# Smaller TensorE parts for two sets of products, and one multiplication on ScalarE instead of GpSimd, in a hybrid RWKV-7 / HGRN2 step

## The chip, the cores and the metric

The kernel runs on one core of one Trainium2 chip. The metric is the time of one execution on the device in microseconds (us). The core has five engines with queues of their own: TensorE (PE, its weight loads are shown apart as PEld), VectorE (DVE), ScalarE (ACT), GpSimd (POOL) and SyncE (SP), which issues the transfers.

## The reference, cut to what matters

One layer serves a prompt of 256 tokens and 8 samples of 8 tokens each, so 320 columns of tokens in all. A combined projection of the normalised input feeds an RWKV-7 branch (16 heads of 64) and an HGRN2 branch (8 heads of 128). The change lies in the two recurrences:

```
# HGRN2, per head: S_t = diag(g_t) S_{t-1} + k_t v_t^T,   o_t = S_t^T q_t
att = einsum('nhtd,nhsd,nhtsd->nhts', qc, kc, decay_ts)       # causal, decayed q.k products
o   = einsum('nhtd,nhde->nhte', qc * exp(b), s) + einsum('nhts,nhse->nhte', att, vc)
s   = exp(b_last)[..., None] * s + einsum('nhsd,nhse->nhde', kc * exp(b_last - b), vc)

# RWKV-7, per head: S_t = S_{t-1} diag(w_t) - (S_{t-1} kk_t)(kk_t * a_t)^T + v_t k_t^T,  y_t = S_t r_t
```

After the layer come a gated merge, an output projection, a residual and a final norm. Both groups' new states are outputs too.

## The kernel before

The channels lie on partitions and the tokens on the free dimension. Large projections are made of float32r products of 128x128 weights with 320 tokens; each weight block (128 columns of 1024 rows) is loaded from memory, cast to its high part on ScalarE (`whi`) and its low part is subtracted on VectorE (`wlo`), and 8 x 3 products use it (`mps`). Weights have three buffers.

From 29 to 718 us of the execution a recorder is at work. `record_all` writes down all operations of 68 projection tiles (3264 `mps` products), of 8 RWKV pairs (`rwkv`, two heads each) and of 8 HGRN heads (`hgrn`). `Recorder.order` then plans the order for each engine from estimated costs, with `mps` products between the small ones, and replays it; in the trace all of it has the line of the replay, L1396, so places are told by their tiles. Small products in PSUM tiles `a` belong to `rwkv`, those in `b` to `hgrn`. They are float32 products, and the trace shows each as two passes, so two rows per product. After 718 us the remaining projections follow, untouched by the change.

Of `rwkv` the change touches the pair products (lines 868 to 878): for each of four 64-token chunks of the prompt, and for the samples, one product of `bk2[:, ci]` (128 channels of two heads by 128 columns) with `arp[:, ci]` (256 columns: for each head a part that is zero in the other head's 64 rows). VectorE multiplies them by a mask into `g2`.

Of `hgrn` it touches the attention scores inside the prompt (lines 1168 to 1267). Blocks of 8 tokens have scores of their own (`k0`, `q0`), and levels of 8, 16, 32 and 64 tokens join neighbouring blocks (`level(sz)` gives one `kq` tile). `products` makes 128x128 products of which only the parts near the diagonal count:

```
for j in range(2):
    tk_ = slice(128 * j, 128 * j + 128)
    T.matmul(ps[:, o_ + 128 * j:o_ + 128 * j + 128], kq[:, tk_], q_[:, tk_], start=True, stop=True)
```

`keep` copies the parts into `att` under a mask (`copy_predicated`). The samples have a product of 64 columns of their own. Their old states `s0` (128x1024 per head) meet the queries in 8 products with 32 columns each (`qz`, lines 1221 to 1224), four of which fill the array side by side. Then line 1245 multiplies `s0` by the decay `dec` on GpSimd in one operation, line 1252 adds the new part, and line 1253 stores it from SP's queue, behind which weight loads wait.

Of the kernel before, what the change touches and what calls it, by code (L numbers as in the profile page):

```python
# [9 lines left out]
F32 = mybir.dt.float32  # L10
F32R = mybir.dt.float32r
U8 = mybir.dt.uint8
# [5 lines left out]
NP_ = 256  # L18
# [30 lines left out]
class Op:  # L49
    __slots__ = ("eng", "fn", "args", "kw", "cost", "lat", "uses", "mode", "passes", "cols", "stream",  # L50
                 "succ", "npred", "ready", "rank", "block", "margin", "wait", "port", "hold", "dma", "n")

# [16 lines left out]
class Recorder:  # L69
# [3 lines left out]
    def __init__(self, engines, is_big):  # L73
        self.real, self.ops, self.spans, self.is_big = engines, [], {}, is_big
        self.block, self.wait = None, 0

# [8 lines left out]
    def add(self, eng, name, fn, args, kw):  # L85
# [18 lines left out]
        o.mode = None  # L104
        o.block = self.block
        o.margin, o.wait = 0, self.wait
# [4 lines left out]
        if eng == "PE":  # L111
# [12 lines left out]
            stream = n / 2.4 + 13 if one and lhs.dtype == F32R else 2 * n / 2.4  # L124
            o.cost = o.passes * max(load, stream / min(2, 128 // o.mode[1]))
            if o.mode == (128, 128) and n > 256:
# [27 lines left out]
    def link(self):  # L154

        writers, readers = {}, {}
        for o in self.ops:
            o.succ, pred = [], {}
            for name, p0, p1, m, wr, psum in o.uses:
# [22 lines left out]
            o.npred = len(pred)  # L182
            for q, data in pred.values():
                q.succ.append((o, data))
        for o in reversed(self.ops):
            o.rank = o.cost + max((q.rank + (o.lat if data else 0) for q, data in o.succ), default=0)

    def order(self):
# [85 lines left out]
def hybrid_step(ctx, tc, x_prompt, x_sample, state_rwkv, state_hgrn, state_shift, norm_g, w_in,  # L274
# [19 lines left out]
    def ctile(shape, name, dt=F32, pool=rconst):  # L294
        return pool.tile(shape, dt, name=name, tag=name)
# [59 lines left out]
    with tc.tile_pool(name="start", bufs=1) as st, \  # L355
# [100 lines left out]

        mf = st.tile([64, 3, 64], F32, name="mf")
        mu8 = ctile([128, 3, 64], "mu8", U8)
        G.memset(mf, 1.0)
        for n, sz in enumerate((8, 8, 16)):  # L460
            if n == 0:
                mfh = mf[:, 0].rearrange("p (b i) -> p b i", i=8)
                keep_ge(mf[:, 0], [[1, 64]], 0, -1)
                keep_ge(mfh, [[-8, 8], [0, 8]], 0, 1)
                keep_ge(mfh, [[8, 8], [0, 8]], 7, -1)
                continue
            lv = mf[:, n].rearrange("p (b two s) -> p b two s", two=2, s=sz)
            nb = 32 // sz
# [3 lines left out]
        for sl in HS:  # L472
            G.tensor_copy(mu8[sl], mf)

# [210 lines left out]
    def ring(pool, tag, shape, bufs, dt, size, clear=False):  # L685
# [12 lines left out]
        if len(shape) == 2:  # L698
# [4 lines left out]
    SIZES = {"uK": 384, "uS": 384, "uE": 384, "uA": 320, "uB": 384, "uQ": 320, "big": 512, "s0t": 512, "v": 384,  # L703
             "w1": 384, "w2": 320, "w3": 320, "ks": 128, "ket": 256}


    CLEAR = {"uB", "uE", "ys", "rhs", "rhs2", "k3", "vm", "w1", "vt"}

# [50 lines left out]
    def rwkv(p, r, k, vp, za):  # L759
# [107 lines left out]
        M = at("M", (128, 3, 2, 64), tag="uE")  # L867
        for g in range(3):
            ps = aps("pg")
            n = 2 if g < 2 else 1  # L870
            for c_ in range(n):
                ci = 2 * g + c_
                T.matmul(ps[:, 256 * c_:256 * c_ + 256], bk2[:, ci].rearrange("p j t -> p (j t)"),
                         arp[:, ci].rearrange("p x h t -> p (x h t)"), start=True, stop=True)
            m = mk[:, 0:2] if g < 2 else mk[:, 2:3]
            V.tensor_mul(g2[:, 2 * g:2 * g + n].rearrange("p c x h t -> p (c x) h t"),
                         ps[:, :256 * n].rearrange("p (a h t) -> p a h t", h=2, t=64),
                         m.rearrange("p c x t -> p (c x) t")[:, :, None].to_broadcast([128, 2 * n, 2, 64]))

# [245 lines left out]
    def hgrn(hd, q, k, v, zb):  # L1125
# [42 lines left out]
        att = bt("att", (128, 2 * 128 + 64))  # L1168
        G.memset(att, 0.0)

        def level(sz, tag):
            half = lambda t_: t_[:, :NP_].rearrange("p (b two s) -> p b two s", two=2, s=sz)
            kq = bt("kq", (128, NP_), tag=tag)
            if sz in (32, 64):

                side = [kq[:, 128 * x:128 * x + 128].rearrange("p (b s) -> p b s", s=sz) for x in range(2)]
            else:
                side = [half(kq)[:, :, x] for x in range(2)]
            for x, e in enumerate((R, F)):
# [9 lines left out]


        def products(ps, o_, kq, q_):
            for j in range(2):
                tk_ = slice(128 * j, 128 * j + 128)
                T.matmul(ps[:, o_ + 128 * j:o_ + 128 * j + 128], kq[:, tk_], q_[:, tk_], start=True, stop=True)

        def keep(ps, o_, n):
            own = lambda t_, c_: t_.rearrange("p (j c t) -> p j c t", c=2, t=64)[:, :, c_]
            for c_ in range(2):
                sl = HS[c_]
                V.copy_predicated(own(att[sl, :NP_], c_), mu8[sl, None, n].to_broadcast([64, 2, 64]),  # L1200
                                  own(ps[sl, o_:o_ + NP_], c_))

        kq8 = level(8, "w2")
        ps = bps("pg")
        products(ps, 0, k0, q0)
        products(ps, 256, kq8, kq8)
        keep(ps, 0, 0)
        keep(ps, 256, 1)

# [10 lines left out]
        ps = bps("pos")  # L1220
        for si in range(NSEQ):
            j = si % 4
            T.matmul(ps[32 * j:32 * j + 32, 128 * (si // 4):128 * (si // 4) + 128], qz[:, si, :], s0[:, si, :],
                     start=True, stop=True)
        sot = bt("sot", (128, 256), tag="ket")
        S.copy(sot, ps[:, :256])
        ps = bps("pke")
        T.matmul(ps[:, 128:192], k0[:, NP_:], q0[:, NP_:], start=True, stop=True)
        T.transpose(ps[0:64, :128], es[:, 1], ident)
        V.copy_predicated(att[0:64, NP_:], mu8[0:64, 0], ps[0:64, 128:192])  # L1230
        k3 = bt("k3", (128, 2, 128), dt=F32R)
# [30 lines left out]
        for j in range(2):  # L1262
            for b in range(2):
                o_ = 64 * j + 32 * b
                V.tensor_copy(att[64 * b:64 * b + 32, 128 * j + 64 * b + 32:128 * j + 64 * b + 64],
                              ps[o_:o_ + 32, 256 + o_:288 + o_])
            V.tensor_copy(att[0:64, 128 * j + 64:128 * j + 128], ps[HS[j], 384 + 64 * j:448 + 64 * j])

# [42 lines left out]
    def shift_state():  # L1311
        for g, (s_, n) in enumerate(((0, 5), (5, 4))):
# [265 lines left out]
```

## Time and profile before

| | us |
|---|---|
| median of 3 runs (1156.60 to 1157.67) | 1157.26 |
| the profiled execution | 1155.96 |
| its span | 1154.3 |
| PE busy | 1135.7 (98%) |
| DVE busy | 775.9 (67%) |
| ACT busy | 669.2 (58%) |
| POOL busy | 208.0 (18%) |

Busy time is an average over the stages, and matmuls overlap in the records, so what a product costs is read from the distance between the starts of the records around it. "Idle before" and the waits tell what an engine waited for. TensorE's granted clock is 1.00 (2.4 GHz) in the whole stretch that the change touches.

### The profile page before, as it was taken

The numbers are of one execution on the slowest core, as the hardware profiler recorded it, in microseconds if no ns is written. First come the engines' busy times: TensorE is split into PE (matmuls) and PEld (weight loads), VectorE is DVE, ScalarE is ACT, GpSimd is POOL, SyncE is SP. The second block draws the span as 40 slices with busy tenths as digits, with TensorE's granted clock in tenths as the row PEclk, the third lists the DMA queues.
The fourth block names the chain that finished last, engine by engine and source line by source line (L and its number), as shares of the span: only waits on it lengthen the run. The fifth ranks groups of instructions, "written<-read, shape, count | busy, mean of one in ns | idle before, by whom it ended". The sixth has DMA issues, their size and how long they took to land.

```text
span 1154.3 us, 20774 instructions
## 1 busy us (share of the span) xinstructions
PE 1135.7 (98%) x7816; PEld 1097.9 (95%) x7816; DVE 775.9 (67%) x1634; ACT 669.2 (58%) x1483; POOL 208.0 (18%) x405
## 2 busy tenths in 40 slices
PE   6999999999999999999999999999999999999997
PEld 6999999999999999999999999999999999998886
DVE  8778878877887888878788686544444444436632
ACT  6766766667666667567667667444444444435322
POOL 9432223222311321421321310000000000000000
PEclk9999999999999999999999999999999999999999
DMA  6745435535445435436435434555555555577512
GB/s 180 199 117 127 129 102 136 142 92 132 129 113 146 117 93 150 131 81 169 120 93 162 115 105 132 148 152 153 152 147 148 151 154 151 146 253 254 182 41 91
DMA packets 283096, 159.69 MB, mean 138 GB/s; under 512 B 22893, under 2 KB 273264, under 8 KB 282356
## 3 DMA queue, kind: packets, MB, share of 16 engines
q1 hardware_dynamic: 282996, 158.37, 48.6%
q8 instruction: 61, 1.00, 0.4%
q14 instruction: 39, 0.32, 0.1%
HBM read 148.53 MB, written 9.81 MB: 137 GB/s over the span
## 4 chain that ended last, share of the span: by engine, by line
PE 96%; POOL 2%; DVE 1%; ACT 1%; issue 0%; DMA 0%; ACTq 0%; POOLq 0%
PE mps L1396 41%; PE a L1396 13%; PE mps L338 6%; PE mps L340 6%; PE mps L339 6%; PE b L1396 4%; PE po L1479 3%; PE po L1481 3%; PE po L1480 3%; PE ppb L338 2%; PE ppa L338 2%; PE ppb L340 2%; PE ppa L340 2%; PE ppa L339 2%; PE ppb L339 2%; PE po L1484 1%
## 5 line engine op out<-in xcount | busy, mean ns | idle before, releaser
L1396 PE MATMUL mps<-hhi,wlo 128*128 128x320 f32 x1088 | 344.9, 317 | 0.0
L1396 PE MATMUL mps<-hlo,whi 128*128 128x320 f32 x1088 | 344.7, 317 | 0.0
L1396 PE MATMUL mps<-hhi,whi 128*128 128x320 f32 x1088 | 344.6, 317 | 0.0
L1396 PEld LDWEIGHTS mps<-hlo,whi 128*128 128x128 f32 x1088 | 204.9, 188 | 3.3 <-issue 3.0
L1396 PEld LDWEIGHTS mps<-hhi,wlo 128*128 128x128 f32 x1088 | 205.0, 188 | 2.7 <-issue 2.4
L1396 PEld LDWEIGHTS mps<-hhi,whi 128*128 128x128 f32 x1088 | 205.0, 188 | 0.8 <-issue 0.4
L329 DVE TENSOR_TENSOR wlo<-raw,whi 128x1024 fp32r<-128x1024 f32 x88 | 107.8, 1225 | 125.0 <-ACT whi L328 124.8
L328 ACT CAST whi<-raw 128x1024 fp32r<-128x1024 f32 x88 | 92.3, 1048 | 163.3 <-PE mps L339 104.8
L1396 ACT CAST whi<-raw 128x1024 fp32r<-128x1024 f32 x134 | 140.6, 1049 | 77.2 <-PE mps L1396 75.8
L1396 DVE TENSOR_TENSOR wlo<-raw,whi 128x1024 fp32r<-128x1024 f32 x134 | 167.5, 1250 | 24.4 <-ACT whi L1396 23.1
L339 PE MATMUL mps<-hlo,whi 128*128 128x320 f32 x448 | 138.5, 309 | 0.0
L338 PE MATMUL mps<-hhi,whi 128*128 128x320 f32 x448 | 138.5, 309 | 0.0
L340 PE MATMUL mps<-hhi,wlo 128*128 128x320 f32 x448 | 138.5, 309 | 0.0
L340 PEld LDWEIGHTS mps<-hhi,wlo 128*128 128x128 f32 x448 | 84.1, 188 | 0.0
L338 PEld LDWEIGHTS mps<-hhi,whi 128*128 128x128 f32 x448 | 84.1, 188 | 0.0
L339 PEld LDWEIGHTS mps<-hlo,whi 128*128 128x128 f32 x448 | 84.1, 188 | 0.0
L1468 DVE TENSOR_TENSOR wlo<-raw,whi 128x1024 fp32r<-128x1024 f32 x32 | 38.5, 1222 | 39.1 <-ACT whi L1467 39.0
L1467 ACT CAST whi<-raw 128x1024 fp32r<-128x1024 f32 x32 | 33.1, 1051 | 48.4 <-DMA raw<-in_w_out_dram 22.4
L1479 PE MATMUL po<-whi,mhi 128*128 128x512 f32 x128 | 50.1, 391 | 0.7 <-DVE gbt L1436 0.7
L1481 PE MATMUL po<-wlo,mhi 128*128 128x512 f32 x128 | 50.0, 391 | 0.0
L1480 PE MATMUL po<-whi,mlo 128*128 128x512 f32 x128 | 50.0, 391 | 0.0
L339 PE MATMUL ppb<-ybl,whi 128*128 128x320 f32 x128 | 39.6, 309 | 0.0
(409 smaller groups left out, 2304.0 us busy)
## 6 DMA issues: line engine op xcount, KB each, us to landing
raw<-in_w_in_dram SPq DMA_DIRECT2D x194, 512.0 KB
raw<-in_w_out_dram SPq DMA_DIRECT2D x32, 512.0 KB
raw<-in_proj_a_dram SPq DMA_DIRECT2D x16, 512.0 KB
raw<-in_proj_b_dram SPq DMA_DIRECT2D x16, 512.0 KB
s<-in_state_hgrn_dram SPq DMA_DIRECT2D x8, 512.0 KB
out_dram<-s SPq DMA_DIRECT2D x8, 512.0 KB
s<-in_state_rwkv_dram SPq DMA_DIRECT2D x8, 256.0 KB
out_dram<-s SPq DMA_DIRECT2D x8, 256.0 KB
```

The lines of the kernel that those rows point to most:

```text
L328: S.copy(hi[:, ks], raw[:, ks])
L329: sub.tensor_sub(lo[:, ks], raw[:, ks], hi[:, ks].bitcast(F32))
L338: T.matmul(dst, hi[:, q, :], xhi[:, k, :], start=(k == 0), stop=False)
L339: T.matmul(dst, hi[:, q, :], xlo[:, k, :], start=False, stop=False)
L340: T.matmul(dst, lo[:, q, :], xhi[:, k, :], start=False, stop=(k == nk - 1))
L1396: o.fn(*o.args, **o.kw)
L1467: S.copy(hi, raw)
L1468: V.tensor_sub(lo, raw, hi.bitcast(F32))
L1479: T.matmul(pt, h, hi, start=first, stop=False)
L1480: T.matmul(pt, l, hi, start=False, stop=False)
L1481: T.matmul(pt, h, lo, start=False, stop=end)
L1484: T.matmul(pt, h, hi, start=first, stop=False)
```

## The change

Three things are done. (1) The scores of all levels are computed in parts of 32 columns (32x32 tiles of scores, 64 wide at the level of 64) right behind the `qz` products, in one group that the planner keeps together (`side_by_side` sets `group`; a member waits for what any member waits for, and all have the highest rank). `products` and `keep` go; the parts of blocks of 8 and levels of 8 and 16 are gathered under masks in a small tile `attc` and copied to `att` by ScalarE. `att` is cleared once for all heads. (2) The pair products of the four chunks are made by head: 64 rows of the array for each head, 128 columns, into one PSUM bank per head, also as a group. (3) `s0` is multiplied by `dec` on ScalarE in 8 operations of 128x128. The planner's cost for a group divides by the tiles that run side by side. The cut diff:

```diff
@@ Recorder.add
+            side = 128 // o.mode[1] * (128 // o.mode[0] if o.group else 1)
+            o.cost = o.passes * max(max(load, stream) / side, 7) if o.group else o.passes * max(load, stream / min(2, side))
@@ Recorder.link
+            for o in members:
+                preds[o.n].update(shared)
...
+            top = max(o.rank for o in members)
@@ rwkv
-        for g in range(3):
-            ps = aps("pg")
-            n = 2 if g < 2 else 1
-            for c_ in range(n):
-                ci = 2 * g + c_
-                T.matmul(ps[:, 256 * c_:256 * c_ + 256], bk2[:, ci].rearrange("p j t -> p (j t)"),
-                         arp[:, ci].rearrange("p x h t -> p (x h t)"), start=True, stop=True)
...
+        banks = [aps("pg") for _ in HS]
+        side_by_side([((banks[h][:, 128 * ci:128 * ci + 128], bk2[HS[h], ci].rearrange("p j t -> p (j t)"),
+                        arp[HS[h], ci, :, h]), dict(start=True, stop=True)) for ci in range(4) for h in range(2)])
...
+        T.matmul(ps[:, :256], bk2[:, 4].rearrange("p j t -> p (j t)"), arp[:, 4].rearrange("p x h t -> p (x h t)"),
+                 start=True, stop=True)
@@ hgrn
-        G.memset(att, 0.0)
-        products(ps, 0, k0, q0)
-        products(ps, 256, kq8, kq8)
-        keep(ps, 0, 0)
-        keep(ps, 256, 1)
+        kq8, kq16, kq32, kq64 = level(8, "w2"), level(16, "o"), level(32, "ket"), level(64, ("s1", "ks"))
...
+        work = [((ps[32 * j:32 * j + 32, 128 * g:128 * g + 128], qz[:, 4 * g + j], s0[:, 4 * g + j]))
+                for g in range(2) for j in range(4)]
+        tile32 = lambda g, c0, a_, b_: work.append((pg[32 * g:32 * g + 32, c0:c0 + b_.shape[-1]], a_, b_))
+        for n, (a_, b_) in enumerate(((k0, q0), (kq8, kq8), (kq16, kq16))):
+            for j in range(2):
+                for g in range(4):
+                    tk_ = slice(128 * j + 32 * g, 128 * j + 32 * g + 32)
+                    tile32(g, 64 * n + 32 * j, a_[:, tk_], b_[:, tk_])
+        for g in range(4):
+            tile32(g, 192, kq32[0][:, 32 * g:32 * g + 32], kq32[1][:, 32 * g:32 * g + 32])
+        for g in range(4):
+            tile32(g, 224, kq64[0][:, 32 * g:32 * g + 32], kq64[1][:, 64 * (g // 2):64 * (g // 2) + 64])
+        for g in range(2):
+            tk_ = slice(NP_ + 32 * g, NP_ + 32 * g + 32)
+            tile32(g, 288, k0[:, tk_], q0[:, tk_])
+        side_by_side([(x_, dict(start=True, stop=True)) for x_ in work])
+        attc = bt("attc", (128, 2, 32))
+        for n in range(3):
+            V.copy_predicated(attc, mu8[:, None, n].to_broadcast([128, 2, 32]),
+                              pg[:, 64 * n:64 * n + 64].rearrange("p (j t) -> p j t", t=32))
+        for g in range(4):
+            own = slice(32 * g, 32 * g + 32)
+            S.copy(att[own, :NP_].rearrange("p (j t) -> p j t", j=2)[:, :, own], attc[own])
+            if g < 2:
+                V.copy_predicated(att[own, NP_ + 32 * g:NP_ + 32 * g + 32], mu8[own, 0], pg[own, 288:320])
...
-        G.tensor_mul(s0, s0, dec[:, :, None].to_broadcast([128, NSEQ, 128]))
+        for si in range(NSEQ):
+            S.activation(s0[:, si], s0[:, si], AF.Copy, scale=dec[:, si:si + 1])
...
-        kq16, kq32, kq64 = level(16, "w3"), level(32, "w2"), level(64, "w1")
-        ps = bps("pl")
-        products(ps, 0, kq16, kq16)
-        T.matmul(ps[:, 256:384], kq32[:, 0:128], kq32[:, 128:256], start=True, stop=True)
-        T.matmul(ps[:, 384:512], kq64[:, 0:128], kq64[:, 128:256], start=True, stop=True)
-        keep(ps, 0, 2)
@@
+    def side_by_side(products):
+        book.group = len(book.ops)
+        for args, kw in products:
+            T.matmul(*args, **kw)
+        book.group = None
```

The order of the instructions shows where this lands. On PE, around the first pair's products, before the change (`a` is a PSUM tile of `rwkv`, the number behind it the buffer):

```order
L1396 MATMUL mps<-hhi,wlo 128x320
L1396 MATMUL a_485<-arp,bk_0_493 128x256
L1396 MATMUL a_483<-arp,bk_0_493 128x256
L1396 MATMUL a_485<-arp,bk_0_493 128x256
L1396 MATMUL a_483<-arp,bk_0_493 128x256
L1396 MATMUL a_484<-arp,bk_0_493 128x256
L1396 MATMUL mps<-hhi,whi 128x320
```

The same place with the change; the replay's line is now L1426:

```order
L1426 MATMUL mps<-hhi,wlo 128x320
L1426 MATMUL a_487<-arp,bk_0_495 128x128
L1426 MATMUL a_485<-arp,bk_0_495 128x128
L1426 MATMUL a_487<-arp,bk_0_495 128x128
L1426 MATMUL a_485<-arp,bk_0_495 128x128
L1426 MATMUL a_487<-arp,bk_0_495 128x128
L1426 MATMUL a_485<-arp,bk_0_495 128x128
L1426 MATMUL a_487<-arp,bk_0_495 128x128
L1426 MATMUL a_485<-arp,bk_0_495 128x128
L1426 MATMUL mps<-hhi,whi 128x320
L1426 MATMUL mps<-hlo,whi 128x320
L1426 MATMUL a_486<-arp,bk_0_495 128x256
```

Eight products alternate between the banks of the two heads where four stood, and the samples' product follows apart. On PE, the group of the first HGRN head with the change (`b` is a PSUM tile of `hgrn`; `w`, `o`, `ket`, `ks` and `s_0_531` hold the `kq` tiles; before, only the `qz` row stood between its neighbours):

```order
L1426 MATMUL b_522<-s_0_518,qz 32x128 x8
L1426 MATMUL b_521<-w_0_527,w_0_519 32x32 x8
L1426 MATMUL b_521<-w_0_526 32x32 x8
L1426 MATMUL b_521<-o_529 32x32 x8
L1426 MATMUL b_521<-ket_530 32x32 x4
L1426 MATMUL b_521<-ks_532,s_0_531 32x64 x4
L1426 MATMUL b_521<-w_0_527,w_0_519 32x32 x2
L1426 MATMUL a_485<-big_516,uv_494 64x512
```

The 9 products (8 of 128 columns and the samples' one of 64) that stood at five other places of the head are now the 34 small ones behind `qz`. On ACT, between two weight casts of the first head, with the change (`s_0_518` is `s0`):

```order
L1426 CAST whi<-raw 128x1024
L1426 COPY zb_477<-mps 128x320
L1426 ACTIVATE uv_494<-a_487 64x64
L1426 ACTIVATE s_0_518<-s_0_518,dec_534 128x128 x2
L1426 COPY ket_530<-b_522 128x256
L1426 ACTIVATE s_0_518<-s_0_518,dec_534 128x128 x2
L1426 ACTIVATE w_0_527<-R_525 128x128
L1426 ACTIVATE w_0_519<-R_525 128x128
L1426 ACTIVATE s_0_518<-s_0_518,dec_534 128x128
L1426 CAST k_0_536<-b_522 32x128 x4
L1426 ACTIVATE s_0_518<-s_0_518,dec_534 128x128 x3
L1426 COPY att_528<-attc_535 32x2x32 x4
```

Eight more operations on `s0` and four copies to `att` stand there. Six more instructions follow before the next weight cast.

## Rows read from the trace of the kernel before

**Rows 1.** The page: the chain that ended last, by engine and by line.

```profile
PE 96%; POOL 2%; DVE 1%; ACT 1%; issue 0%; DMA 0%; ACTq 0%; POOLq 0%
PE mps L1396 41%; PE a L1396 13%; PE mps L338 6%; PE mps L340 6%; PE mps L339 6%; PE b L1396 4%; PE po L1479 3%; PE po L1481 3%; PE po L1480 3%; PE ppb L338 2%; PE ppa L338 2%; PE ppb L340 2%; PE ppa L340 2%; PE ppa L339 2%; PE ppb L339 2%; PE po L1484 1%
```

**Rows 2.** Busy time by stretch, us; sum of nine, 30 to 718 us.

```profile
core 0: us, PE busy (x) PEld busy (x) DVE busy (x) ACT busy (x) POOL busy (x), PEclk, DMA share, GB/s
...
118.00:200.00 82.00, 82.00 (x605) 80.17 (x604) 67.24 (x166) 55.77 (x142) 22.30 (x42) 1.00 0.47 125
...
612.00:695.00 83.00, 83.00 (x610) 81.11 (x609) 64.23 (x160) 54.19 (x136) 18.62 (x33) 1.00 0.45 126
...
sum 688.00, PE 686.98 PEld 671.57 DVE 556.08 ACT 465.13 POOL 179.83; mean PE 76.33 PEld 74.62 DVE 61.79 ACT 51.68 POOL 19.98
```

**Rows 3.** Waits of PE and PEld, 29 to 720 us: total, times, longest.

```profile
PE a L1396 <- DVE ast L1396: 0.6, 1, 0.6
...
PEld mps L1396 <- issue: 5.9, 11, 0.8
```

**Rows 4.** PE in order of time, level products: start us, us, engine, line, work.

```profile
90.09 0.60 PE L1396 MATMUL b<-w,w 128*128 128x128 f32 x4
90.54 0.61 PE L1396 MATMUL a<-pp,uB 128*128 128x128 f32 x4
```

**Rows 5.** The same view, the samples' own product of a later head.

```profile
669.64 0.33 PE L1396 MATMUL b<-w,w 128*128 128x64 f32 x2
669.81 0.27 PE L1396 MATMUL b<-ident,es 128*64 128x128 f32 x1
```

**Rows 6.** The same view, the first pair's pair products.

```profile
62.69 0.31 PE L1396 MATMUL mps<-hhi,wlo 128*128 128x320 f32 x1
62.84 2.32 PE L1396 MATMUL a<-arp,bk 128*128 128x256 f32 x10
...
65.14 0.31 PE L1396 MATMUL mps<-hlo,whi 128*128 128x320 f32 x1
```

**Rows 7.** The same view, the last head's old-state products (qz).

```profile
676.05 0.31 PE L1396 MATMUL mps<-hhi,whi 128*128 128x320 f32 x1
676.29 0.64 PE L1396 MATMUL b<-s,qz 128*32 128x128 f32 x16
676.86 0.41 PE L1396 MATMUL mps<-hlo,whi 128*128 128x320 f32 x1
677.11 0.38 PE L1396 MATMUL a<-ident,sr 128*128 128x128 f32 x2
```

**Rows 8.** First qz, starts from 100.75 to 100.80 us; all qz, ns.

```profile
100.75 0.32 PE L1396 MATMUL b<-s,qz 128*32 128x128 f32 x4
...
L1396 PE MATMUL b<-s,qz x128: 272/273/298, 100.8 to 676.7; 128*32 128x128 f32 x128
```

**Rows 9.** PE in order of time, two 64-column products on separate halves.

```profile
101.32 0.64 PE L1396 MATMUL a<-big,uv 128*64 128x512 f32 x1
101.33 0.64 PE L1396 MATMUL a<-s0t,uv 128*64 128x512 f32 x1
101.80 0.59 PE L1396 MATMUL a<-big,uv 128*64 128x512 f32 x1
```

**Rows 10.** Single operations: count, ns min/median/max (CAST: busy us, mean ns).

```profile
L1396 POOL TENSOR_TENSOR s<-s,dec x8: 1889/1918/2069, 101.5 to 677.0; 128x1024 f32<-128x1024 f32 x8
...
L1396 ACT ACTIVATE sf<-st,f x24: 387/402/416, 100.3 to 696.4; 128x128 f32<-128x128 f32 x24
...
L1396 ACT CAST v<-vt 32x128 fp32r<-32x128 f32 x32 | 9.5, 296 | 0.7
...
L1396 DVE COPY_PREDICATED att<-mu,b x56: 214/296/313, 92.0 to 683.2; 64x128 f32<-64x128 uint8 x48, 64x64 f32<-64x64 uint8 x8
```

**Rows 11.** Waits of ACT and of SP's queue: total us, times, longest us.

```profile
ACT whi L1396 <- PE mps L1396: 75.8, 79, 2.1
...
SPq L1396 <- DVE s L1396: 49.2, 11, 12.2
```

More of the change, by code (lines that the diff above doesn't have):

```diff
@@ L50 @@
     __slots__ = ("eng", "fn", "args", "kw", "cost", "lat", "uses", "mode", "passes", "cols", "stream",
-                 "succ", "npred", "ready", "rank", "block", "margin", "wait", "port", "hold", "dma", "n")
+                 "succ", "npred", "ready", "rank", "block", "margin", "wait", "port", "hold", "dma", "n", "group")
 def span_of(ap):
@@ L74, in __init__ @@
         self.real, self.ops, self.spans, self.is_big = engines, [], {}, is_big
-        self.block, self.wait = None, 0
+        self.block, self.wait, self.group = None, 0, None
     def proxy(self, eng):
@@ L104, in add @@
         o.mode = None
-        o.block = self.block
+        o.block, o.group = self.block, self.group
         o.margin, o.wait = 0, self.wait
@@ L181, in link @@
             pred.pop(o.n, None)
-            o.npred = len(pred)
-            for q, data in pred.values():
+        groups = {}
+        for o in self.ops:
+            if o.group is not None:
+                groups.setdefault(o.group, []).append(o)
+        for members in groups.values():
+            own = {o.n for o in members}
+            shared = {}
+            for o in members:
+                for n, (q, data) in preds[o.n].items():
+                    if n not in own:
+                        shared[n] = q, data or shared.get(n, (q, False))[1]
+            for o in members:
+                preds[o.n].update(shared)
+        for o in self.ops:
+            o.npred = len(preds[o.n])
+            for q, data in preds[o.n].values():
                 q.succ.append((o, data))
@@ L186, in link @@
             o.rank = o.cost + max((q.rank + (o.lat if data else 0) for q, data in o.succ), default=0)
+        for members in groups.values():
+            top = max(o.rank for o in members)
+            for o in members:
+                o.rank = top
     def order(self):
@@ L471, in hybrid_step @@
             keep_ge(lv[:, :, 1, :], [[2 * sz, nb], [0, sz]], sz - 1, -1)
-        for sl in HS:
-            G.tensor_copy(mu8[sl], mf)
+        for g in range(4):
+            G.tensor_copy(mu8[32 * g:32 * g + 32], mf)
         junk = st.tile([128, D], F32, name="junk")
@@ L703, in hybrid_step @@
     SIZES = {"uK": 384, "uS": 384, "uE": 384, "uA": 320, "uB": 384, "uQ": 320, "big": 512, "s0t": 512, "v": 384,
-             "w1": 384, "w2": 320, "w3": 320, "ks": 128, "ket": 256}
-    CLEAR = {"uB", "uE", "ys", "rhs", "rhs2", "k3", "vm", "w1", "vt"}
+             "w1": 384, "w2": 320, "w3": 320, "ks": 128, "ket": 256, "o": NT}
+    CLEAR = {"uB", "uE", "ys", "rhs", "rhs2", "k3", "vm", "w1", "vt", "att", "attc"}
     def at(name, shape=(128, NT), tag=None, bufs=1, dt=F32):
@@ L1168, in hgrn @@
         att = bt("att", (128, 2 * 128 + 64))
-        G.memset(att, 0.0)
         def level(sz, tag):
             half = lambda t_: t_[:, :NP_].rearrange("p (b two s) -> p b two s", two=2, s=sz)
-            kq = bt("kq", (128, NP_), tag=tag)
             if sz in (32, 64):
-                side = [kq[:, 128 * x:128 * x + 128].rearrange("p (b s) -> p b s", s=sz) for x in range(2)]
+                half_ = bt("kq", (128, NP_), tag=tag) if sz == 32 else None
+                kq = [half_[:, 128 * x:128 * x + 128] for x in range(2)] if sz == 32 else \
+                    [bt("kq", (128, 128), tag=t_) for t_ in tag]
+                side = [x.rearrange("p (b s) -> p b s", s=sz) for x in kq]
             else:
+                kq = bt("kq", (128, NP_), tag=tag)
                 side = [half(kq)[:, :, x] for x in range(2)]
@@ L1188, in level @@
             return kq
[L1191 to L1204, printed above, removed]
-        products(ps, 0, k0, q0)
-        products(ps, 256, kq8, kq8)
-        keep(ps, 0, 0)
-        keep(ps, 256, 1)
+        kq8, kq16, kq32, kq64 = level(8, "w2"), level(16, "o"), level(32, "ket"), level(64, ("s1", "ks"))
         es = bt("es", (128, 2, 64))
@@ L1220, in hgrn @@
         ps = bps("pos")
[L1221 to L1224, printed above, removed]
+        pg = bps("pg")
+        work = [((ps[32 * j:32 * j + 32, 128 * g:128 * g + 128], qz[:, 4 * g + j], s0[:, 4 * g + j]))
[18 more added lines that the diff above has]
+                              pg[:, 64 * n:64 * n + 64].rearrange("p (j t) -> p j t", t=32))
+        for g in range(4):
+            own = slice(32 * g, 32 * g + 32)
+            S.copy(att[own, :NP_].rearrange("p (j t) -> p j t", j=2)[:, :, own], attc[own])
+            if g < 2:
+                V.copy_predicated(att[own, NP_ + 32 * g:NP_ + 32 * g + 32], mu8[own, 0], pg[own, 288:320])
+        for j in range(2):
+            for b in range(2):
+                V.tensor_copy(att[64 * b:64 * b + 32, 128 * j + 64 * b + 32:128 * j + 64 * b + 64],
+                              pg[64 * j + 32 * b:64 * j + 32 * b + 32, 192:224])
+            V.tensor_copy(att[0:64, 128 * j + 64:128 * j + 128], pg[HS[j], 224:288])
         sot = bt("sot", (128, 256), tag="ket")
@@ L1227, in hgrn @@
         ps = bps("pke")
-        T.matmul(ps[:, 128:192], k0[:, NP_:], q0[:, NP_:], start=True, stop=True)
         T.transpose(ps[0:64, :128], es[:, 1], ident)
-        V.copy_predicated(att[0:64, NP_:], mu8[0:64, 0], ps[0:64, 128:192])
         k3 = bt("k3", (128, 2, 128), dt=F32R)
```

33 lines of the change are left out of this document (15 added, 18 removed).

## The prediction, made before the changed kernel was run

> **What bounds the kernel now.** I read the chain of waits first. 96% of the chain that ended last is TensorE work, and POOL, DVE and ACT have 4% together [rows 1]. Then the stretch from 30 to 718 us, the only one that the change touches: of 688 us PE is busy for 687, DVE for 556, ACT for 465 and POOL for 180, at the full clock [rows 2]. Third, PE's waits there: the largest for data is 0.6 us, and 5.9 us of gaps have no releaser at all [rows 3]. So PE's order is full from end to end, the other engines have room, and nobody's latency is waited for. The time of this stretch is a sum of what each product takes on PE, and this is what I work out. The 436 us behind it are the same in both kernels.
>
> **Level products, before.** The first four passes of 128 columns start at 90.09 and the next product at 90.54: 0.112 us per pass [rows 4]. A head has 8 such products in two passes each: 16 x 0.112 = 1.79 us. The samples' two passes of 64 columns take 669.81 - 669.64 = 0.17 us [rows 5]. Sum 1.96 us per head, all on PE's path.
>
> **Level products, after.** 34 products, so 68 passes. How such parts run is seen in `qz`, 32 columns of weights and 128 moving columns. Of its 16 passes four start within 0.05 us of each other [rows 8], and the set of 16 spans 0.64 us from the first start to the last end [rows 7]; less the last one's 0.27 [rows 8] the starts span 0.37. Less the 0.02 that four starts take (0.32 - 0.30, [rows 8]), four sets follow at about 0.11: a set of four runs side by side, and a set takes what one pass takes for its 128 moving columns. That is 0.85 ns per column, so 27 ns for a set of 32 and 54 ns for one of 64, if four starts need no more. From rows 8 they need 0.02 for three steps, so 4 x 7 = 28 ns, just as much. Sets: 12 for blocks and levels of 8 and 16, 2 for the level of 32, 2 for the samples (half filled), 2 of 64 columns. 16 x 0.027 + 2 x 0.054 = 0.54 us. Entry and exit of the 32-column mode are paid already, since the parts stand right behind `qz`, and by the order of the instructions TensorE changes into and out of 32 and 64 columns as often as before. **Gain 1.96 - 0.54 = 1.42 us per head, 11.4 us for eight.**
>
> **Pair products.** Before: from 62.69 to 65.14 less two large products of 0.147 lie 2.16 us for ten passes of 256 columns, 0.215 each [rows 6]. After: 16 passes of 128 columns with half the rows each. No row shows two row halves at work together. The nearest rows are two 64-column products on separate halves of the columns: they start 10 ns apart, and the second passes of both start 0.48 us later, so two streams run as one [rows 9]. I take the same for rows: 8 x 0.112 = 0.90. The mode is new here. Going in costs 676.29 - 676.05 - 0.147 = 0.09 us, coming out 676.86 - (676.29 + 0.37) - 0.11 = 0.09, and the first weight load that nothing hides 677.11 - 676.86 - 0.147 = 0.10 [rows 7], which I count on both sides: 0.38. The samples' product stays, 2 x 0.215 = 0.43. Sum 1.71, **gain 0.45 us per pair, 3.6 us for eight.** Bounds: with a free mode change 1.33, gain 6.6 us; with halves one after the other 1.71 + 0.90 = 2.61, loss 3.6 us.
>
> **Other engines.** ACT gets 8 x 0.402 for `s0` and 4 copies of at most 0.296 [rows 10]: 4.4 us per head, 35 us in all, on an engine that is busy for 465 of 688 and that waits 79 times for PE to free a weight buffer [rows 11]; I cost it at nothing, with that cover, and its loss is a rival below. POOL loses 1.92 us per head [rows 10] and the clearing of `att`. DVE loses 48 masked copies of 0.296 and 8 of 0.214 and gets 40 of the shorter kind or less [rows 10], 7 us less in all. Neither was waited for, so nothing is gained there. On SP's queue the store of `s0` moves by one or two weight loads; loads already stood behind state stores for up to 12.2 us [rows 11] without a wait on PE, so nothing again. The mask's smaller set-up at the start is off the path.
>
> **Sum.** 11.4 + 3.6 = 15.0 us. The profiled execution took 1155.96, which gives 1141.0; the median of the runs is 1.3 us higher, and I forecast on that: 1157.26 - 15.0 = **1142.3 us**. At most 1 us of PE's waits is left to win besides.
>
> **Rivals.** *Row halves in series.* Nothing in the trace excludes it. The level gain less 3.6: 7.8 us, 1149.5.
>
> *Passes start no closer than 25 ns.* The 15 steps of `qz` take 0.37 us, 24.7 ns on average [rows 7, 8]. If that were a limit of starting and not of streams, 68 passes would take 1.68 us, the gain would be 0.28 per head, and 2.2 + 3.6 = 5.8 us give 1151.5. Against it stand the four starts within 0.05 us [rows 8]. The Trainium skill (TensorEngine Tiling (Array Packing), section Instruction Overhead) has a rule against this change: about 60 cycles of overhead for each matmul, so that a tiling factor should not be taken from a dimension that is small already. By that rule, as an estimate, a pass costs 25 ns and the result is this rival's; the close starts of `qz` speak against it for parts on different columns, but only for four in a row.
>
> *Slower: TensorE cannot be fed so many small passes.* The place is the group behind `qz`: 84 passes with 84 weight loads in about 1 us, where the densest long run in the trace has one pass in 0.112 us [rows 4]. `qz` is dense but short, and may have been waiting ready behind its semaphore. If the supply ran at 0.112, 68 passes would take 7.6 us: 5.7 us lost per head, 45 in all, less 3.6 from the pairs, so 1199. It decides from (1.96 + 0.45) / 68 = 35 ns per pass on; beyond that the kernel is slower.
>
> *ScalarE is late with weights.* Its queue is in order, and the 4.4 us stand between two weight casts. If the cover were gone, all of 35 us would reach PE, 1177; from 1.9 us per head on the gain is eaten. For it: DVE and ACT are the busiest after PE. Against it: the 79 waits for a buffer, and weights in three buffers, of which each lasts PE 24 x 0.147 = 3.5 us.
>
> *It does nothing that can be measured:* the planner places small products so that gaps open elsewhere, 1155 to 1159.
>
> **Chances.** Forecast 0.62, row halves in series 0.09, 25 ns per pass 0.08, too little supply 0.06, ScalarE late 0.09 (a third of it still faster), nothing 0.06. About 0.2% (2.3 us) is what a measurement can tell from no change. Faster: 0.62 + 0.09 + 0.08 + 0.03 = 0.82; within: 0.06 + 0.01 = 0.07; slower: 0.06 + 0.05 = 0.11. The range begins where the pairs' mode change is free, 1157.3 - 11.4 - 6.6 = 1139.3, less most of the 1 us of waits: 1138.5, and reaches over the row halves and the 25 ns to 1153: 0.62 + 0.09 + 0.08 + 0.03 = 0.82.
>
> **What would show it.** In the profile after: the group spans about 1 us from `qz`'s first start to the first start of the 64-column products, with sets 27 ns apart; if sets stand 100 ns apart, the rule or the supply was right. The pair products span about 0.9 us with starts in twos; single starts 0.11 apart mean series. PE's waits from 29 us on stay below some 8 us in all; a wait of `mps` for `wlo` means that ScalarE is late. The stretch ends some 15 us earlier, near 703, and what follows keeps its length. I am wrong if PE's busy share in the stretch falls or if the later part changes.

## The result, and the profile after

The changed kernel takes **1141.84 us** (median of four runs, 1141.60 to 1142.03), the kernel before 1157.47 (four runs): ratio 0.9864, 95% interval 0.9847 to 0.9881. The profiled execution took 1141.97 us; its page begins:

```profile
span 1140.2 us, 21763 instructions
## 1 busy us (share of the span) xinstructions
PE 1121.6 (98%) x8280; PEld 1084.8 (95%) x8280; DVE 765.5 (67%) x1618; ACT 690.8 (61%) x1579; POOL 191.0 (17%) x393
...
## 4 chain that ended last, share of the span: by engine, by line
PE 96%; DVE 1%; POOL 1%; ACT 1%; issue 0%; DMA 0%; ACTq 0%; DVEq 0%; POOLq 0%
```

PE has the chain as before [rows 1]. The same table by stretch as [rows 2], cut where the replay ends now (PE, PEld, DVE, ACT, POOL busy, then PE's clock, DMA share, GB/s):

```profile
30.00:704.00 674.00, 672.98 (x5494) 658.56 (x5493) 545.97 (x1336) 487.29 (x1271) 163.19 (x335) 1.00 0.46 128
704.00:1140.00 436.00, 427.49 (x2659) 407.74 (x2658) 196.42 (x237) 184.28 (x276) 0.00 (x0) 1.00 0.52 156
```

The stretch is 14 us shorter, PE still fills it up to 1 us, and the 436 us behind it hold the same 427.49 us of PE work as in the kernel before:

```profile
718.00:1154.00 436.00, 427.49 (x2659) 407.74 (x2658) 196.64 (x239) 184.48 (x278) 0.00 (x0) 0.99 0.52 155
```

From the first to the last start of the replay it was 688.98 us and is 674.87: 14.1 us, the whole difference of the spans (1154.3 - 1140.2).

PE in order of time, the last head's group, to set beside [rows 7] (start us, us, engine, line, work):

```profile
666.11 0.31 PE L1426 MATMUL mps<-hhi,whi 128*128 128x320 f32 x1
666.35 0.64 PE L1426 MATMUL b<-s,qz 128*32 128x128 f32 x16
666.81 0.31 PE L1426 MATMUL b<-w,w 128*32 128x32 f32 x16
...
667.31 0.30 PE L1426 MATMUL b<-ks,s 128*32 128x64 f32 x6
667.39 0.24 PE L1426 MATMUL b<-w,w 128*32 128x32 f32 x4
667.57 0.41 PE L1426 MATMUL mps<-hlo,whi 128*128 128x320 f32 x1
667.82 0.38 PE L1426 MATMUL a<-ident,sr 128*128 128x128 f32 x2
```

From `qz`'s first start to the next large product it is now 1.21 us, where `qz` alone took 0.57 (676.86 - 676.29, [rows 7]). So the 68 new passes cost 0.64 us. All eight groups take 1.213 or 1.214 us.

The first pair's products, to set beside [rows 6]:

```profile
62.99 0.31 PE L1426 MATMUL mps<-hhi,wlo 128*128 128x320 f32 x1
63.23 1.16 PE L1426 MATMUL a<-arp,bk 64*128 64x128 f32 x16
64.33 0.41 PE L1426 MATMUL mps<-hhi,whi 128*128 128x320 f32 x1
64.58 0.31 PE L1426 MATMUL mps<-hlo,whi 128*128 128x320 f32 x1
64.72 0.60 PE L1426 MATMUL a<-arp,bk 128*128 128x256 f32 x2
64.97 0.50 PE L1426 MATMUL mps<-hhi,wlo 128*128 128x320 f32 x1
65.31 0.31 PE L1426 MATMUL mps<-hhi,whi 128*128 128x320 f32 x1
```

From 62.99 to 64.58 less two large products of 0.147 is 1.29 us, with both mode changes; the samples' product, apart now, takes 0.44 (from 64.58 to 65.31, less two large products again). In the records the 16 starts come in twos, 6 to 7 ns apart: 63.233 and 63.240, 63.447 and 63.453, and from there a two every 0.112 us. PE's waits from 29 to 706 us, PEld with them, beside [rows 3]:

```profile
PE a L1426 <- DVE ast L1426: 0.8, 1, 0.8
```

```profile
PEld mps L1426 <- issue: 5.7, 7, 0.8
PEld a L1426 <- issue: 2.2, 7, 1.0
PEld b L1426 <- issue: 1.7, 6, 0.8
PEld a L1426 <- POOL yz L1426: 0.7, 2, 0.4
```

No wait of `mps` for `whi` or `wlo` is among them.

### The profile page after: what moved, and what is told of

It reads as the page before. It is cut to its first block, busy times and chain, and to the rows that moved or that the text cites. A ratio compares the mean times of both kernels' runs of the same rounds, so it can differ in the third digit from the quotient of the medians.

```text
span 1140.2 us, 21763 instructions
## 1 busy us (share of the span) xinstructions
PE 1121.6 (98%) x8280; PEld 1084.8 (95%) x8280; DVE 765.5 (67%) x1618; ACT 690.8 (61%) x1579; POOL 191.0 (17%) x393
## 4 chain that ended last, share of the span: by engine, by line
PE 96%; DVE 1%; POOL 1%; ACT 1%; issue 0%; DMA 0%; ACTq 0%; DVEq 0%; POOLq 0%
PE mps L1426 41%; PE a L1426 12%; PE mps L361 6%; PE mps L360 6%; PE mps L359 6%; PE b L1426 3%; PE po L1509 3%; PE po L1511 3%; PE po L1510 3%; PE ppb L361 2%; PE ppa L361 2%; PE ppb L360 2%; PE ppa L360 2%; PE ppa L359 2%; PE ppb L359 2%; PE po L1515 1%
## 5 line engine op out<-in xcount | busy, mean ns | idle before, releaser
L1426 PE MATMUL mps<-hhi,wlo 128*128 128x320 f32 x1088 | 345.3, 317 | 0.0
L1426 PE MATMUL mps<-hhi,whi 128*128 128x320 f32 x1088 | 344.1, 316 | 0.0
L1426 PE MATMUL mps<-hlo,whi 128*128 128x320 f32 x1088 | 343.9, 316 | 0.0
L1426 PEld LDWEIGHTS mps<-hhi,wlo 128*128 128x128 f32 x1088 | 204.9, 188 | 4.1 <-issue 3.2
L1426 PEld LDWEIGHTS mps<-hlo,whi 128*128 128x128 f32 x1088 | 204.9, 188 | 2.2 <-issue 1.6
L1426 PEld LDWEIGHTS mps<-hhi,whi 128*128 128x128 f32 x1088 | 204.9, 188 | 1.5 <-issue 0.8
L1426 ACT CAST whi<-raw 128x1024 fp32r<-128x1024 f32 x134 | 140.3, 1047 | 63.3 <-PE mps L1426 61.3
L1426 DVE TENSOR_TENSOR wlo<-raw,whi 128x1024 fp32r<-128x1024 f32 x134 | 165.2, 1233 | 14.8 <-ACT whi L1426 13.7
L1497 ACT CAST whi<-raw 128x1024 fp32r<-128x1024 f32 x32 | 33.4, 1052 | 48.6 <-PE po L1514 25.0
L359 PE MATMUL ppa<-yah,whi 128*128 128x320 f32 x128 | 39.6, 309 | 0.0
```

What stands on the lines that cost most here:

```text
L359: T.matmul(dst, hi[:, q, :], xhi[:, k, :], start=(k == 0), stop=False)
L1426: o.fn(*o.args, **o.kw)
L1497: S.copy(hi, raw)
```

## The experiments

Ratios are to the kernel before, run on the same chip beside each; its medians there lie between 1156.88 and 1157.47 us, so that a difference between two kernels that were not run beside each other carries these 0.6 us. "The stretch" is the replay, first to last start. A gap is the distance from one start to the next on PE, less what the first product takes for its columns (0.147 us for a large one).

**One part at a time.** Three kernels hold one part of the change each, a fourth all but the move to ScalarE. The edits are blocks of the diff above put back or taken alone; this one is in two of them:

```diff
-        for si in range(NSEQ):
-            S.activation(s0[:, si], s0[:, si], AF.Copy, scale=dec[:, si:si + 1])
+        G.tensor_mul(s0, s0, dec[:, :, None].to_broadcast([128, NSEQ, 128]))
```

Level products alone (the pairs' block and `s0` as before):

> The change with the pair products and the samples' multiplication put back as they were; only the level products in 32-column parts stay. Theory (the stretch is the sum of TensorE's work, so the parts add): in the profile of the changed kernel the group with qz takes 0.64 us more per head than qz alone did, against 1.96 us removed, so 1.32 x 8 = 10.6 us faster than before, a ratio near 0.991. Rival (the time won came from taking the work off GpSimd, or the parts do not add): under 6 us or over 14 us.

Measured: 1147.52 us, ratio 0.9916 (0.9902 to 0.9929), 9.6 us faster. The group takes 1.24 to 1.27 us here, 0.03 to 0.05 more than with the whole change: the same 84 passes, with wider distances between some of the starts; why is not shown. The stretch is 9.4 us shorter.

Pair products alone (the kernel before, with the pairs' block and the planner's groups):

> Only the pair products by head in row halves. Theory: 2.16 us per pair before, 1.73 us in the profile of the changed kernel, 0.43 x 8 = 3.4 us faster than before, a ratio near 0.997. Rival (the mode change costs more when the planner places it elsewhere): no change, within 1 us.

Measured: 1153.96 us, ratio 0.9972 (0.9962 to 0.9983), 3.1 us faster. The block of 16 passes takes the same 1.29 us, and the samples' product apart 0.42 to 0.44 (0.53 where it stands right behind the block, whose 0.10 for the first weight load is then counted twice). The stretch is 2.2 us shorter and not 3.4, because the new order has more gaps, the largest a wait of PE for VectorE:

```profile
PE a L1426 <- DVE uv L1426: 1.0, 1, 1.0
```

The move to ScalarE alone (the kernel before, with the edit above turned round):

> Only the samples' old states multiplied on ScalarE, 8 operations per head. Theory (no engine but TensorE is waited for): within 1.5 us of before, and PE's waits from 29 us on stay under 10 us. Rival one (GpSimd's operation of 1.9 us held DVE's port, so taking it away wins time): 3 us faster or more. Rival two (ScalarE is late with the weights): 3 us slower or more, with waits of mps for wlo.

Measured: 1159.92 us, ratio 1.0022 (1.0013 to 1.0032), **2.8 us slower**. That is between what the two theories said, and the waits of PEld for ACT show that it is neither:

```profile
PEld b L1397 <- ACT v L1397: 1.6, 2, 0.8
PEld a L1397 <- ACT uv L1397: 1.4, 2, 0.7
PEld b L1397 <- ACT ket L1397: 1.2, 3, 0.4
```

Small products wait for ACT's results: such waits of PEld add up to 4.8 us, and the three largest stand here. The kernel before has one of them:

```profile
PEld b L1396 <- ACT v L1396: 0.8, 1, 0.8
```

Nothing waits for weights. ScalarE has the time but not always the right moment: with 3.2 us more per head between its other operations some results come later. The planner's order has changed as well, and what it does to the waits was not taken apart.

The whole change with `s0` on GpSimd again:

> The change with the samples' multiplication back on GpSimd. Theory: the two TensorE parts give all of it, so 14 us faster than before, within 1.5 us of the changed kernel. Rival (the move to ScalarE is needed for the gain, since with TensorE shorter GpSimd's multiplication comes late for the adds and the store behind it): 3 us or more slower than the changed kernel.

Measured: 1142.42 us, ratio 0.9872 (0.9859 to 0.9886), stretch 675.08 us: 0.6 us above the changed kernel, with intervals that overlap. Its eight groups take 1.27 us instead of 1.21, which is 0.4 of it. With the rest of the change in place the move is worth nothing that can be told. The parts alone add up to -9.6 - 3.1 + 2.8 = -9.9 us, the whole is -15.6. Of these 5.7 us the traces show 4.0: the gaps over 0.25 us add up to 2.3, 2.9 and 2.9 us in the three partial orders and to 1.5 before and after the whole change, which makes 3.6, and the groups of the level products alone are 0.4 us longer. The rest was not found.

**Do the row halves run side by side?**

```diff
-  arp[HS[h], ci, :, h]), dict(start=True, stop=True)) for ci in range(4) for h in range(2)])
+  arp[HS[h], ci, :, h]), dict(start=True, stop=True)) for h in range(2) for ci in range(4)])
```

> The changed kernel with the eight pair products issued head after head: four on one row half, then four on the other, instead of in turns. Theory (two row halves run at the same time only when their products stand next to each other): the group of a pair takes about 0.8 us longer than its 1.29 us, so 6 to 7 us slower than the changed kernel, about 1148.5. Rival (TensorE takes the other half's products out of turn, or the halves were never at work together): the pair's group keeps its 1.29 us and the time its 1142.

Measured: 1144.85 us, ratio 0.9894 (0.9877 to 0.9911), 3.0 us above the changed kernel; the block takes 1.84 us instead of 1.29:

```profile
63.01 0.31 PE L1426 MATMUL mps<-hhi,wlo 128*128 128x320 f32 x1
63.25 1.71 PE L1426 MATMUL a<-arp,bk 64*128 64x128 f32 x16
64.89 0.41 PE L1426 MATMUL mps<-hhi,whi 128*128 128x320 f32 x1
65.14 0.31 PE L1426 MATMUL mps<-hlo,whi 128*128 128x320 f32 x1
```

So side by side is real, and the order of issue is part of it. The loss is 0.55 us and not the 0.8 of eight passes, because the second head's first pass starts at 63.805 us, 5 ns after the first head's fifth of eight: half of the work still overlaps. By the groups that is 8 x 0.55 = 4.4 us; 3.0 remain in the time, since PEld's gaps without a releaser are 1.6 us smaller in this order (8.0 in all, against 9.6).

**Is ScalarE near its limit?** The eight operations of a head are cut into 32 of a quarter of the size:

```diff
+            for c0 in range(0, 128, 32):
-            S.activation(s0[:, si], s0[:, si], AF.Copy, scale=dec[:, si:si + 1])
+                S.activation(s0[:, si, c0:c0 + 32], s0[:, si, c0:c0 + 32], AF.Copy, scale=dec[:, si:si + 1])
```

> The changed kernel with the samples' old states multiplied in 32 operations of 32 columns per head instead of 8 of 128: by the 0.40 us of one of 128 columns, about 0.3 us each, so some 6 to 7 us more of ScalarE per head, 50 us in all. Theory (ScalarE has room for the casts, and the planner puts them first): weights still come in time, under 4 us slower than the changed kernel. Rival (ScalarE late): mps waits for wlo or whi, 10 us slower or more.

Measured: 1142.95 us, ratio 0.9880 (0.9865 to 0.9894). ACT's busy time grows by 34 us (690.8 to 724.8) and not by 50, the stretch by 0.4 us (675.23); it starts 0.9 us later. ScalarE's cover takes 34 us more.

**What does the planner's group carry?**

```diff
-        book.group = len(book.ops)
+        book.group = None
```

> The changed kernel without the planner's group: the same products at their own ranks and with the old cost rule. By the order of the instructions the old-state products then stand in turns with the small parts, and TensorE changes its mode 50 times instead of 44. Theory (a change into and out of a mode costs 0.2 us each): 1 to 3 us slower than the changed kernel. Rival (parts that alternate with wide products on the same columns lose most of the side-by-side work): the group takes 0.4 us or more longer per head, 4 us slower or more.

Measured: 1153.20 us, ratio 0.9967 (0.9955 to 0.9978): **11.4 us above the changed kernel**, far more than expected. The passes are not to blame: the 84 of a head take 0.9 us more in all eight heads together. PEld's largest waits for another engine are:

```profile
PEld b L1426 <- ACT ket L1426: 4.1, 4, 1.4
PEld a L1426 <- POOL ys L1426: 1.7, 4, 0.6
```

Without the group the planner prices a small pass as if at most two ran side by side, and a member waits for its own inputs only. It then puts other things in places where their inputs are late: gaps over 0.25 us add up to some 9 us against 1.5 with the group. With the 0.9 that is 8.5 of the 11.1 us by which the stretch is longer; the rest was not found. A group also gives all its members the highest rank; which of these rules carries how much was not tried.

**Can TensorE be fed?** The small products of a head are issued twice, then three times, with the same values (one line, twice shown):

```diff
-        side_by_side([(x_, dict(start=True, stop=True)) for x_ in work])
+        side_by_side([(x_, dict(start=True, stop=True)) for x_ in work + work[NSEQ:]])
```

> The changed kernel with every 32-column part of the level products issued twice, the second time with the same result: 34 more products per head in the group, 76 in a row. Theory (starts every 8 ns per pass whatever the length of the run): 68 more passes take 0.55 us per head, 4.4 us in all, about 1146.5. Rival (a queue that was full before the group hides a slow supply, and runs empty in a longer group): passes further and further apart towards the end of the group, up to 0.112 us each, and 10 us or more slower than the changed kernel.

Measured: 1153.56 us, ratio 0.9970 (0.9959 to 0.9982), 11.7 us above the changed kernel. The groups grow by 0.639 us each, 9.4 ns per pass exactly as for the first 68, so 5.1 us in all. The other 6.6 us lie outside them, 3 of them in one place, which the waits of PE name without a releaser:

```profile
PE a L1426 <- issue: 2.8, 1, 2.8
```

It stands behind the group that ends at 435.5 us. Another part of the 6.6 us is TensorE's clock. Just behind this gap, from 439.0 to 442.4 us, the granted clock is at its lower level (1.2 GHz, 0.50 in the last but two column):

```profile
439.10:442.30 3.20, 3.20 (x15) 3.13 (x14) 2.42 (x12) 2.06 (x8) 0.61 (x2) 0.50 0.02 5
```

In these rows large products start 0.27 us apart (439.97, 440.24, 440.51) instead of 0.147, so 3.4 us there cost, as an estimate, 3.4 x (1 - 0.147 / 0.267) = 1.5 us. A threefold issue (`work + 2 * work[NSEQ:]`) was to show whether that is an accident:

> The 34 small products of a head are issued three times, with the same result, so 220 passes stand in a row. Inside the group all theories expect 9.4 ns for each added pass: 1.21 + 2 x 0.64 = 2.49 us, 10.2 us more for eight heads. They differ outside it. In the kernel that issued them twice one gap of 3.1 us without a releaser stood right behind a group, and a 16 KB packet on an instruction queue ended 1.3 us before it ended. Theory one: PE runs out of instructions there, because the packets of 16 KB hold 256 instructions each (17,648 of PE's in that kernel, 69 packets) and come late behind weight transfers. Then 440 instructions in 2.5 us meet it more often: at least three gaps of over 1 us without a releaser, each within 5 us of a group and each with an instruction packet landing inside it, and over 10 us of loss outside the groups. Theory two: the gap was an accident of the order that the planner chose; then gaps over 1 us are rare, stand anywhere, have a releaser, and the loss outside the groups stays at about 7 us or below.

Measured: 1180.08 us (1175.51 to 1182.29), ratio 1.0202 (1.0185 to 1.0219), slower than the kernel before. The profiled execution is the one of 1175.51. Its waits of PE from 29 to 740 us begin:

```profile
PE b L1426 <- issue: 17.4, 8, 3.5
```

In order of time, one of these is in the middle of the first head's group:

```profile
105.61 0.31 PE L1426 MATMUL b<-o 128*32 128x32 f32 x10
108.10 0.23 PE L1426 MATMUL b<-o 128*32 128x32 f32 x3 [2.18 <-issue]
```

The records of the transfers have 16 KB on the instruction queue q8 from 105.44 to 106.85 us. PE goes on 1.25 us after that. These are that queue's packets in the changed kernel and in the threefold one:

```profile
q8 instruction: 65, 1.06, 0.4%
```

```profile
q8 instruction: 73, 1.20, 0.4%
```

The changed kernel has 2 x 8280 PE instructions on its page, 64.7 times 256; the threefold one 2 x 9368, 73.2 times. So q8 is PE's own queue, and a packet holds 256 instructions. From the records I counted how many of PE's instructions (weight loads, products and some 140 others, semaphores above all) had started when a packet had landed, less 256 for each packet before it:

| kernel | median | largest values | longest of the gaps, us |
|---|---|---|---|
| before | 193 | 278, 251, 248 | under 1 |
| changed | 196 | 356, 316, 296 | under 1 |
| small ones twice | 198 | 449, 447, 436 | 3.1, 0.8, 0.5 |
| three times | 201 | 449 seven times, 377, 373 | 3.6, 3.0, 2.5, 2.3, 2.3, 2.1, 1.9 |

The count never goes over 449, and at each of the seven 449s PE stands still and goes on 1.2 to 1.5 us after the landing. The same records can be read the other way round. Numbered by their starts from 0, the record 449 + 256 x k needs packet k, when the packets are numbered from 0 too. In the threefold kernel such a record ends each of the eight stops, the eighth included (1.0 us at 270.5, whose packet landed before it began): it starts 1.20 to 1.46 us after its packet's landing. In the kernel with the small ones twice it ends the three gaps of the table, 1.30 to 1.32 us after the landing. Elsewhere in the four kernels of the table these records come later: the next nearest is 1.9 us behind its packet, without a gap, and in the changed kernel the nearest is 2.4 us behind. That is theory one as far as the instructions go: PE had used up what was there. The missing 63 to two packets (512) would have to be instructions without a record that ran before the first stop, since the number is the same in the first stop, at 106 us, and in the last, at 696 us; that was not tried. Seven of the eight stops stand inside a group, and so does most of the loss, which the expectation had put outside. What makes a packet late is taken up at the end.

After or in three of the eight stops the clock falls, too:

```profile
360.50:363.70 3.20, 3.20 (x15) 3.08 (x14) 2.62 (x12) 2.85 (x12) 0.00 (x0) 0.50 0.39 89
534.60:537.80 3.20, 2.76 (x11) 2.72 (x11) 0.12 (x1) 1.02 (x5) 0.00 (x0) 0.50 0.00 0
701.90:705.10 3.20, 3.20 (x14) 3.10 (x13) 1.90 (x9) 3.05 (x12) 0.00 (x0) 0.50 0.00 0
```

This makes the sum whole. The threefold kernel's stretch is 33.5 us longer than the changed kernel's: 10.2 for the passes, 18.7 for the eight stops, and 3 x 1.5 for the clock are 33.4. With the small ones twice it is 11.8 us longer: 5.1, 4.4 for three stops and 1.5 for the clock are 11.0.

**A version that beats both.** The samples' product goes into row halves too, each into a bank of its own:

```diff
+        last = [aps("pg"), bps("pg")]
+        place = lambda h, ci: banks[h][:, 128 * ci:128 * ci + 128] if ci < 4 else last[h][:, 0:128]
...
-                        arp[HS[h], ci, :, h]), dict(start=True, stop=True)) for ci in range(4) for h in range(2)])
+                        arp[HS[h], ci, :, h]), dict(start=True, stop=True)) for ci in range(5) for h in range(2)])
...
-        T.matmul(ps[:, :256], bk2[:, 4].rearrange("p j t -> p (j t)"), arp[:, 4].rearrange("p x h t -> p (x h t)"),
-                 start=True, stop=True)
...
```

> The samples' product of a pair is made in row halves too, in the same group, each half into a bank of its own: ten products of 128 columns in five twos. My theory (two halves share one stream): a fifth two takes 2 x 0.112 = 0.22 us where the product apart took 0.437, so 0.21 us less for each pair, 1.7 us for eight, about 0.2% faster than the changed kernel, and the group in the trace grows from 1.29 to 1.51 us. Rival: the group now waits for four free banks at once, one of which belongs to the HGRN heads; then PE's waits for banks grow by more than 1.7 us and the time is the same as the changed kernel's or slower.

Measured: **1140.38 us** (1140.03 to 1140.47, four runs), ratio 0.9852 (0.9837 to 0.9866). All its runs lie below all of the changed kernel's, by 1.5 us at the median, though the intervals of the ratios overlap (the kernel before took 1157.42 us beside it). The stretch is 2.4 us shorter (672.46). Its gaps over 0.25 us add up to 0.5 instead of 1.5, so 1.4 are left for the blocks where 1.7 were expected. The first pair's group:

```profile
64.62 0.31 PE L1425 MATMUL mps<-hlo,whi 128*128 128x320 f32 x1
64.86 1.27 PE L1425 MATMUL a<-arp,bk 64*128 64x128 f32 x17
...
65.97 0.27 PE L1425 MATMUL b<-arp,bk 64*128 64x128 f32 x1
66.17 0.42 PE L1425 MATMUL mps<-hhi,wlo 128*128 128x320 f32 x1
66.42 0.31 PE L1425 MATMUL mps<-hhi,whi 128*128 128x320 f32 x1
```

From 64.62 to 66.42 less 0.294 is 1.51 us, as expected; and the wait for four banks does not show: PE's only wait for data over 0.2 us in the stretch is one of 0.3.

## Why the prediction was right

1. **PE's order is full and the time is a sum over it: right.** The stretch lost 14.1 us, the parts behind it nothing, and by the groups the sum is 8 x (1.32 + 0.43) = 14.0. The forecast 1142.3 is 0.5 us above the median, and that it is so near is in part luck: the sum of 15.0 is 1.0 too high, while the medians differ by 15.6. The profiled executions, 1155.96 and 1141.97, differ by 14.0; the one before stood 1.3 us below its median, the one after 0.1 above.

2. **Level products: right mechanism, one term a little small.** 68 passes at 0.54 us were forecast, 0.64 were measured, so the gain is 1.96 - 0.64 = 1.32 per head, 10.6 us and not 11.4. The term that was mis-sized is the set of four 32-column parts at 27 ns. In the records of the last head the first such sets come 29 to 32 ns apart, with four starts in 20 ns and a pause of 9 to 12; later two passes start every 16.7 ns, 33 for four. From the first (666.813) to the first product of 64 columns (667.277) that is 0.46 us against 14 x 0.027 = 0.38 forecast. The parts of 64 columns and the samples' take 0.16 to the last start, as forecast (0.108 + 0.054). What holds the 32-column sets at 31 to 33 ns, the starts or the streams, was not told apart.

3. **Pair products: right.** 1.29 + 0.44 = 1.73 us against 1.71, so the gain is 0.43 per pair, 3.4 us. The price of the mode (0.38) was taken from `qz` [rows 7] and held for row halves: 1.29 less 8 x 0.112 leaves 0.39.

4. **Other engines at nothing: right for this change, with the cover that was named.** Putting `s0` back on GpSimd changes nothing that can be told, and 34 us more on ScalarE cost 0.4 us in the stretch. The new operations' records add up to 32.9 us, against 35 forecast, and what ACT waits for PE to free a weight buffer falls from 75.8 us [rows 11] to 61.3:

```profile
ACT whi L1426 <- PE mps L1426: 61.3, 57, 3.8
```

Not every order leaves it so: alone, the move costs 2.8 us. One sign was set too low. PE's waits were to stay below some 8 us; with PEld's the largest groups add up to 12.0 us, but in the kernel before it was 12.4, so they have not grown.

5. *Row halves in series* is refuted by the starts in twos and by the order head after head, which is 0.55 us slower. *Passes start no closer than 25 ns* is refuted by rows of the changed kernel: 68 passes in 0.64 us. By the overhead of about 60 cycles per matmul (the Trainium skill, TensorEngine Tiling (Array Packing), section Instruction Overhead) they would take, as an estimate, 1.7 us; the trace does not agree where neighbours stand on different columns of the array. *ScalarE late with weights* is refuted by the 32 operations per head; the price that it has in a bad order is on results, not on weights. *It does nothing that can be measured* did not come true for the whole change, but its mechanism shows in the kernels with one part each: their gaps are 0.8 to 1.4 us larger.

6. *TensorE cannot be fed* did not come true here, but it is a real mechanism with another threshold than the forecast had. The added passes cost 9.4 ns each in a group of 152, as the first 68 did in one of 84, and 9.8 in the one group of 220 that was not stopped; there is no slow rate of 0.112 us. What runs out is the stock of instructions: at 152 passes per group PE ran dry three times, at 220 eight times, and then the kernel is slower than before, as that rival said. The changed kernel came as far as 356 of 449. The Trainium skill (Runtime: NRT & Kernel Launch, section Instruction fetch mechanics) says that instructions come in blocks of 16 KiB, 256 of them, which the packets show, and that fetching is hidden; with the threefold products it is not, by 17.4 us.

7. What the forecast did not see: 11 us of the gain hang on the planner's group. It costed the products as they were ordered, and that order is itself made by the group's rules.

## What to carry to other kernels

Where TensorE's order is full, cut products whose result counts only near a diagonal into 32-column parts, keep all parts in one block so that the mode is paid once, and price a part by its start, some 8 ns per pass here, and not by its columns. Let two row halves alternate in the order of issue, each with a bank of its own (one bank for both was not tried), and bring every product of that shape into the same block. Count the instructions too: some 170 per block passed freely here, 300 began to run the queue dry, and 440 cost more than the parts had gained, a part of it through the clock behind the stops.

## What the runs showed of the hardware that was not expected

- Passes on different 32-column parts of the array, each with its own weight load, start about 8 ns apart for as long as instructions last, for 32 moving columns each; some 16 ns apart for 64. All kinds together it is 9.4 ns per pass, in blocks of 84 and of 152.
- Two 64-row halves start 6 to 7 ns apart and share the time of one stream, 0.112 us for 128 columns in float32. Issued half after half, the second half starts just behind the fifth of the first half's eight passes, so before the last three.
- PE stops when 449 of its recorded instructions beyond the last packets have started, and needs 1.2 to 1.5 us after the next packet's landing to go on. The packets themselves take about 1 us (0.9 to 1.4), before a stop as elsewhere; what varies is when they start. In six of the eight stops the weights' transfers kept all DMA engines busy until at most 1.5 us before the packet's start; before the other two (the second and the third, 1.9 and 1.0 us long) the DMA engines stood idle. These are the 3 us before the packets of the second stop and of the seventh (DMA share and GB/s are the last two columns):

```profile
183.90:186.90 3.00, 3.00 (x132) 2.81 (x133) 2.45 (x6) 1.63 (x7) 1.09 (x3) 1.00 0.00 0
615.40:618.40 3.00, 2.70 (x185) 2.46 (x184) 1.20 (x3) 2.01 (x6) 0.31 (x1) 1.00 1.26 277
```

So a stop does not need the weights' transfers. That they make a packet start later, and a stop longer, is read from the order of events and was not tried by itself.

- In four cases TensorE's granted clock fell from 1.00 to 0.50 for 3.4 us, each time in or within 1.8 us behind a stop of 2.1 to 3.6 us. After other stops of up to 3.0 us it stayed at 1.00, so what decides is not shown.
